# A tuned hybrid decoder layer: first-stage copies a tile ahead, a third buffer for sample states, gate weights split ahead, two FFN sums in other homes

## The chip, the cores and the metric

The kernel runs on one core of one Trainium2 chip. The metric is the device time of one execution in microseconds (us). The core has TensorE (PE: matmuls, and PEld: its weight loads), VectorE (DVE), ScalarE (ACT) and GpSimd (POOL), which compute, and SyncE (SP), which here only issues DMAs. POOL and ACT issue DMAs too. The instructions of one engine run in the order in which the program lists them; engines wait for each other through semaphores.

## What is computed

The reference is one inference step of one decoder layer, for a prompt of 512 new tokens and for 8 samples of one token each, with D = 2048, all in float32:

```
proj = rmsnorm(x, norm_mix_g) @ w_in      # columns: bg, cg, h (1024 each), q, k (512 each),
                                          # v, og (1024 each), glr (16)
ya = bg * causal_conv3(cg * h)            # 1024 channels
logf = log_sigmoid(glr @ gate_w2 + gate_b) / 16
S_t = diag(exp(logf_t)) S_{t-1} + k_t^T v_t ;  o_t = q_t S_t      # 4 heads, dk 128, dv 256
yb = rmsnorm(o, gla_norm_g) * silu(og)
x = x + concat(ya, yb) @ w_out
u, v = split(rmsnorm(x, norm_ffn_g) @ w_up)                       # 5632 channels each
x = x + (silu(causal_conv3(u) + b) * v) @ w_down
y = rmsnorm(x, final_norm_g)
```

The samples start from given states (two rows of each convolution, one S per sample and head), the prompt from zero states. The outputs are y and the new states.

## The kernel before, in words

**Layout.** Activations lie transposed, features on the 128 partitions, T = 520 tokens (512 of the prompt, 8 samples) along the row. A feature tile of x is a 128 x 520 block; there are 16 (KD). Every float32 operand of a matmul is split into two parts, hi = the value rounded to the reduced type fp32r (ACT) and lo = the rest (DVE), and a product is three matmuls: hi·hi, hi·lo, lo·hi. Weights come in pieces of 128 x 1024 floats (`load`, L98, on SP's queue; `parts`, L106, makes hi with ACT at L110 and lo with DVE at L111). The pools for raw, hi and lo pieces have three buffers each. `tmp()` (L91) gives one of eight temporaries. A `group` (L170) is one output tile of the projection: two pieces, 96 matmuls, and between quarters of it a `tick()` that emits one step of queued work.

**Order.** The instructions are placed on the engines by a scheduler. `InOrder` (L57) fixes their order in a region to the order of the program text: PE, DVE and ACT, and POOL or SP where they are named. In the first stage it holds PE, DVE, ACT and POOL; from L1575 on, POOL and SP as well. In between, the scheduler chooses.

**First stage (L276 to L491).** x arrives by rows and is transposed tile by tile. `x_tile(k)` (L367) transposes tile k on PE into one of two PSUM buffers, copies it to a temporary (ACT for k < 4, then DVE, L374 and L376), splits it with the norm's weight (L379 or L381, through `split`, L120, instructions at L125 and L126) and stores the copy to `xT_d` (L382, on SP). The loop at L434 runs over the 16 tiles: the matmuls of tile k for head 0's k and q columns, then `x_tile(k + 2)`. Beside it the squares of x are summed (tile column 0 on POOL and DVE, L448 and L449, the others on ACT, L451; the samples' in four pieces, L457), and the low-rank gate's weights, the states' rows and the parameters are loaded. Behind the loop stand the row norms (L467 to L470), `state_columns` (L417, eleven small transposes at L420 and four copies), the gate's matmuls over 12 tiles, the norms spread over partitions into R (L478 to L486), the gate over the other 4 tiles, and the masks for the heads (`make_masks`, L255, on POOL).

**Heads and convolution tiles (L740 to L1060).** For each of four heads: groups for k, q and v (two tiles), then a convolution tile of three groups (`conv_tile`, L755). The attention of a head (`gla_head`, L816) runs in steps at the ticks of later groups. Seven levels give the scores (L923 takes a level's product L, made by POOL, ACT and DVE). `sample_pair` (L884) loads two samples' states (`s0`, two buffers, L886) and their v rows, updates the states (L896) and stores them; `sample_out` (L905, matmul at L909) uses them two steps later. At the end of a head stands the norm of its output: a sum over partitions, a logarithm and an exponential on ACT, and a Newton step of four operations (`newton`, L237), on POOL for heads 0 to 2 and on DVE for head 3. In `conv_tile` the product z is made on POOL for tiles 0 to 2 (L765). After an odd tile, `mixed_done` (L745) forms sums of the tile and the even one before it, splits them and stores them.

**Gate (og), mix, output and FFN stages.** Two og groups follow (L1588 to L1619). Then all products use a scheme of seven products of half tiles (order 1, 5, 6, 2, 7, 3, 4) in place of eight; the sums of activations that it needs are `forms`, kept in 16 home slots, each a pair of hi and lo tiles (`form`, L648). 9 mix groups, 8 output groups ("wo"), 44 "up" and 20 "down" groups follow, each of seven products. `begin` (L1132) and `load_rest` load weights, `prepare` (L1143) splits a product's weights two products ahead (L1158 and L1162). During the last output group, earlier computed sums of the residual are loaded back (`load_sum`, L1534, on SP) and split in half steps set by `split_sums` (L1541); the loads are issued at the products listed at L1701. The first product of the up groups needs PSUM banks that the output groups' sums have just left (L1444 reads the last).

## Time and profile before

| | us |
|---|---|
| median of 3 runs | 2208.77 |
| the runs | 2207.36, 2208.77, 2214.17 |
| profiled execution | 2213.88 |
| its span on the core | 2212.1 |
| mean granted TensorE clock | 0.991 |

The profile is of one execution. A group row names line, engine, operation, what is written and read, count, then busy us and mean ns. A wait row says which line waited for which, with the total in us, the number of waits and the longest. A timeline row has the start in us, the duration, the engine, and in brackets the idle time ahead of it with what ended it; an engine with q is its queue of issued DMAs. A windows row has the length of the window, the busy us of PE, PEld, DVE, ACT and POOL with counts of instructions, the granted clock as a share of full speed, the share of time in which the 16 DMA engines moved data, and GB/s. A DMA row has its count, the size, and the median us from issue to landing. The clock of TensorE is granted by a throttle; 0.50 means half speed.

### The profile page before, as it was taken

How to read it: one execution, taken by the hardware profiler on the slowest of the kernel's cores; microseconds unless marked ns; L12 is line 12 of the kernel's file. 1: busy time of each engine (PE TensorE's matmuls, PEld its weight loads, DVE VectorE, ACT ScalarE, POOL GpSimd, SP SyncE). 2: the span in 40 equal slices, each digit the busy share in tenths (PEclk: the TensorE clock that was granted, in tenths of full speed). 3: DMA queues.
4: the chain of work that ended last, by engine and by line, in shares of the span. 5: the costliest groups of instructions: out<-in, count | busy, mean ns of one | idle time of the engine just before them, and what ended most of it. 6: DMA issues, size and time to landing. Idle time of an engine off the chain costs nothing.

```text
span 2212.1 us, 43799 instructions
## 1 busy us (share of the span) xinstructions
PE 2161.8 (98%) x17751; PEld 2136.8 (97%) x17751; DVE 1734.8 (78%) x2291; ACT 1112.8 (50%) x1629; POOL 444.6 (20%) x620
## 2 busy tenths in 40 slices
PE   7999999999999998999999999999999999999997
PEld 6999999989999998999999999999999999999997
DVE  5355463759887898989898899898988778888876
ACT  5345344335554476555555555555555553444444
POOL 3023241311223511112212121122121310010000
PEclk9999999999999999999999999999999999999999
DMA  8344454367788998666667667666677877894734
GB/s 244 108 132 127 134 176 137 110 204 185 198 215 281 297 247 240 159 174 181 183 163 193 175 168 188 175 181 182 163 193 194 287 189 205 243 273 131 218 110 150
DMA packets 468151, 415.51 MB, mean 188 GB/s; under 512 B 21593, under 2 KB 426357, under 8 KB 467805
## 3 DMA queue, kind: packets, MB, share of 16 engines
q1 hardware_dynamic: 425201, 291.84, 46.2%
q0 software_dynamic: 41424, 118.64, 20.5%
q8 instruction: 139, 2.28, 0.4%
q10 hardware_dynamic: 1324, 2.23, 0.3%
q14 instruction: 63, 0.52, 0.1%
HBM read 299.45 MB, written 80.31 MB: 172 GB/s over the span
## 4 chain that ended last, share of the span: by engine, by line
PE 74%; DVE 4%; DMA 3%; issue 1%; SPq 1%; ACT 1%; ACTq 0%; DVEq 0%
PE mm L1182 34%; PE ms L1182 13%; PE x L1425 7%; PE y L1425 7%; PE mm L139 5%; PE e L1425 3%; PE f L1425 3%; DVE lo L1162 1%; DMA raw<-in_w_out_dram 1%; DMA raw<-in_w_down_dram 1%; DVE acc L1444 1%; DVE yl L123 1%; DVE s L1103 0%; DMA yl<-mt_d 0%; DMA yl<-t_d 0%
## 5 line engine op out<-in xcount | busy, mean ns | idle before, releaser
L1182 PE MATMUL mm<-yh,hi 128*128 128x260 f32 x1696 | 479.9, 283 | 0.7 <-DVE t L597 0.7
L1182 PE MATMUL mm<-yl,hi 128*128 128x260 f32 x1696 | 478.5, 282 | 0.4 <-DVE yl L123 0.4
L1182 PE MATMUL mm<-yh,lo 128*128 128x260 f32 x1696 | 478.2, 282 | 0.3 <-DVE lo L1162 0.3
L1158 ACT ACTIVATE hi<-raw 128x1024 fp32r<-128x1024 f32 x324 | 342.6, 1057 | 231.9 <-PE mm L1182 67.2
L1162 DVE TENSOR_TENSOR lo<-raw,hi 128x1024 fp32r<-128x1024 f32 x324 | 396.0, 1222 | 40.7 <-ACT hi L1158 40.2
L1162 DVE TENSOR_TENSOR lo<-s,hi 128x1024 fp32r<-128x1024 f32 x243 | 298.5, 1228 | 127.6 <-ACT hi L1158 122.3
L1158 ACT ACTIVATE hi<-s 128x1024 fp32r<-128x1024 f32 x243 | 256.8, 1057 | 216.2 <-DVE s L1103 79.8
L1182 PEld LDWEIGHTS mm<-yl,hi 128*128 128x128 f32 x1696 | 319.1, 188 | 0.9 <-DVE yl L123 0.9
L1182 PEld LDWEIGHTS mm<-yh,lo 128*128 128x128 f32 x1696 | 319.3, 188 | 0.6 <-DVE lo L1162 0.6
L1182 PEld LDWEIGHTS mm<-yh,hi 128*128 128x128 f32 x1696 | 318.7, 188 | 1.0 <-issue 0.9
L1182 PE MATMUL ms<-b,hi 128*128 128x260 f32 x1408 | 255.8, 281 | 0.0
L1182 PEld LDWEIGHTS ms<-b,hi 128*128 128x128 f32 x1408 | 216.8, 188 | 0.0
L1425 PE MATMUL x<-form,hi 128*128 128x260 f32 x1120 | 204.6, 283 | 3.0 <-issue 1.7
L1425 PE MATMUL y<-form,hi 128*128 128x260 f32 x1120 | 204.4, 282 | 0.6 <-DVE acc L1444 0.6
L1103 DVE TENSOR_TENSOR s<-s,raw 128x1024 f32<-128x1024 f32 x162 | 198.1, 1223 | 2.8
L1182 PE MATMUL ms<-b,lo 128*128 128x260 f32 x704 | 198.7, 282 | 0.0
L1425 PEld LDWEIGHTS x<-form,hi 128*128 128x128 f32 x1120 | 172.5, 188 | 3.5 <-issue 2.9
L1425 PEld LDWEIGHTS y<-form,hi 128*128 128x128 f32 x1120 | 172.6, 188 | 0.8 <-issue 0.8
L111 DVE TENSOR_TENSOR lo<-raw,hi 128x1024 fp32r<-128x1024 f32 x76 | 95.3, 1258 | 82.2 <-ACT hi L110 75.5
L1425 PE MATMUL y<-form,lo 128*128 128x260 f32 x560 | 158.2, 283 | 0.0
L1425 PE MATMUL x<-form,lo 128*128 128x260 f32 x560 | 158.1, 282 | 0.0
L110 ACT ACTIVATE hi<-raw 128x1024 fp32r<-128x1024 f32 x76 | 79.5, 1051 | 109.2 <-PE mm L139 101.6
(367 smaller groups left out, 5161.9 us busy)
## 6 DMA issues: line engine op xcount, KB each, us to landing
raw<-in_w_up_dram SPq DMA_DIRECT2D x176, 512.0 KB, 4.0
raw<-in_w_down_dram SPq DMA_DIRECT2D x96, 512.0 KB, 6.7
raw<-in_w_in_dram SPq DMA_DIRECT2D x92, 512.0 KB, 4.9
form<-f_d SPq DMA_DIRECT2D x126, 260.0 KB, 6.5
raw<-raw POOLq DMA_DIRECT2D x56, 512.0 KB, 5.4
f_d<-t POOLq DMA_DIRECT2D x80, 260.0 KB, 5.5
raw<-in_w_out_dram SPq DMA_DIRECT2D x32, 512.0 KB, 12.6
form<-g_d POOLq DMA_DIRECT2D x42, 260.0 KB, 7.7
```

What stands on the lines that cost most here:

```text
L110: nc.scalar.activation(hi, raw, AF.Copy)
L111: nc.vector.tensor_tensor(lo, raw, hi.bitcast(F32), op=ALU.subtract)
L123: nc.vector.tensor_tensor(lo, src, hi.bitcast(F32), op=ALU.subtract)
L139: nc.tensor.matmul(o, w, xx, start=first and i == 0, stop=last and i == 2)
L1103: return lambda: nc.vector.tensor_tensor(out, x, y, op=ALU.add)
L1158: nc.scalar.activation(his[i], src, AF.Copy)
L1162: nc.vector.tensor_tensor(los[i], src, his[i].bitcast(F32), op=ALU.subtract)
L1182: nc.tensor.matmul(st["bank"][b], w[:, k, :], x, start=b not in st["used"] and k == 0 and j == 0, stop=k == 7 and j == 2, skip_group_check ...
L1425: nc.tensor.matmul(ps[:, m, :], w[:, k, m * P : (m + 1) * P], x, start=b not in st["used"] and k == 0 and j == 0, stop=k == 3 and j == 2, ...
L1444: nc.vector.tensor_tensor(a, a, inner(bk[b]), op=op)
```

## The change

- First stage: `x_tile` becomes `x_copy` (transposes and copy) and `x_split` (store to `xT_d`, now on POOL and ahead of the split, and the split). From k = 3 on the loop issues the copy of tile k + 3 ahead of the split of tile k + 2.
- The squares: the last tile column's four squares are issued in pairs at k = 14 and 15; the samples' become one instruction over all 2048 columns, in place, at k = 13.
- Head 0's first v weights are loaded at k = 8 and 9; their splits stand at k = 12 and behind the row norms.
- `state_columns` moves behind the gate's last matmuls. The gate runs over 8 tiles ahead of the norms' spreading and 8 behind it (12 and 4 before).
- Heads: the Newton step and the product z are on DVE for all heads. `sample_load` is apart from `sample_pair`; a pair is loaded at the end of the step before, and `s0` has three buffers. The even convolution tile's result stays in the z pad and not in a tile `ye` of the heads' pool.
- At the last convolution tile the order of the program text begins to hold for POOL and SP there and not at L1575, and the first og group's two pieces are loaded and split ahead of that tile's evacuation and sums; `load_og` gives the other two.
- FFN sums: forms (5, 0) and (5, 1) go to home slots 14 and 15 and (7, 2) and (7, 3) to 0 and 1 (they were the other way round); the loads of (5, 0) and (5, 1) are issued at product 0 of the last output group and not at product 1; the split of (4, 2) is half a step earlier. In `load_form`, homes 0 and 7 of the down forms are exchanged.

```diff
+    def group(w, c0, acts, ws=None):
-        ws = [piece(w, k0, 8, c0, P) for k0 in (0, 8)]
+        ws = ws or [piece(w, k0, 8, c0, P) for k0 in (0, 8)]
...
+        def x_copy(k):
             ps = tps()
...
+            st = copies[k] = tmp()[:, :T]
...
+        def x_split(k):
+            st = copies.pop(k)
+            nc.gpsimd.dma_start(xT_d[k], st)
             if k < KD // 2:
...
-            nc.sync.dma_start(xT_d[k], st)
...
+            while upto < min(k + (3 if k < 3 else 4), KD):
+                x_copy(upto)
+                upto += 1
             if k + 2 < KD:
-                x_tile(k + 2)
+                x_split(k + 2)
...
+            elif c < 3:
+                square(c, t)
+            if k in (8, 9):
+                v0.append(load(w_in, (k - 8) * 8, 8, 4096, P))
+            if k == 12:
+                v0[0] = parts(*v0[0])
+            if k == 13:
+                nc.scalar.activation(xs, xs, AF.Square, accum_out=var[:NS, 4:5])
+            if k >= 14:
+                square(3, 2 * k - 28)
+                square(3, 2 * k - 27)
...
-        state_columns()
+        v0[1] = parts(*v0[1])
...
-        low_rank_gate(glr_ps, 0, 12)
+        low_rank_gate(glr_ps, 0, 8)
...
-        low_rank_gate(glr_ps, 12, 4)
+        low_rank_gate(glr_ps, 8, 8)
...
+        state_columns()
         make_masks(sp)
...
-        newton(out, v, t, eng)
+        newton(out, v, t, nc.vector if out is not R else nc.gpsimd)
...
+        if kind == "down" and home in (0, 7):
+            home = 7 - home
...
+    FFN_HOMES = {(5, 0): 14, (5, 1): 15, (7, 2): 0, (7, 3): 1}
...
-            k = {5: 0, 4: 4, 6: 8, 7: 12}[f] + g
+            k = homes.get((f, g), {5: 0, 4: 4, 6: 8, 7: 12}[f] + g)
...
-            eng = nc.gpsimd if j < NH - 1 else nc.vector
-            eng.tensor_tensor(z[:, 2:], cgr[:, :T], hr[:, :T], op=ALU.mult)
+            nc.vector.tensor_tensor(z[:, 2:], cgr[:, :T], hr[:, :T], op=ALU.mult)
...
             ps = group(w_in, j * P, xa)
+            if j == NH - 1:
+
+                in_order = InOrder(nc.gpsimd.engine, nc.sync.engine)
+                ws_og.extend([piece(w_in, k0, 8, 5120, P) for k0 in (0, 8)])
...
-                even[j] = ya = evp[0].tile([P, T], F32, tag="ye", name="ye")
+                even[j] = ya = z[:, 2:]
...
-                def sample_pair(b0):
-                    s0 = gp.tile([P, 2, DV], F32, tag="s0", name="s0", bufs=2)
+                def sample_load(b0):
+                    s0 = gp.tile([P, 2, DV], F32, tag="s0", name="s0", bufs=3)
...
+                    if i < 4:
+                        s0.append(sample_pair(2 * i, *loaded))
                     if 2 <= i < 6:
                         sample_out(2 * i - 4, s0.popleft())
-                    if i < 4:
-                        s0.append(sample_pair(2 * i))
+                    if i < 3:
+                        loaded = sample_load(2 * i + 2)
...
-    raws = [load_og(n) for n in range(3)]
-    ws = [parts(*raws[0])]
-    raws.append(load_og(3))
+    raws = [load_og(2), load_og(3)]
...
-    ws.append(parts(*raws[1]))
-    ps = new_mm()
-    span(ps, ws[0], xa, 0, 0, 8, KD)
-    ws.append(parts(*raws[2]))
-    span(ps, ws[1], xa, 8, 8, 8, KD)
-    ws.append(parts(*raws[3]))
+    ps = new_mm()
+    span(ps, ws_og[0], xa, 0, 0, 8, KD)
+    ws = [parts(*raws[0])]
+    span(ps, ws_og[1], xa, 8, 8, 8, KD)
+    ws.append(parts(*raws[1]))
...
-        for n in (5, 5.5, 6.5, 7, 7.5, 8.5, 9, 9.5, 10):
+        for n in (5, 5.5, 6.5, 7, 7.5, 8, 9, 9.5, 10):
...
-                    1: ((5, 0), (5, 1)), 2: ((5, 2),), 3: ((4, 0), (4, 1)), 4: ((4, 2),),
+                    0: ((5, 0), (5, 1)), 2: ((5, 2),), 3: ((4, 0), (4, 1)), 4: ((4, 2),),
```

More of the change, by code (lines that the diff above doesn't have):

```diff
@@ L365, in trunk_kernel @@
         nc.vector.tensor_copy(gm, ps[:, :16])
-        def x_tile(k):
+        copies = {}
+        def x_copy(k):
             ps = tps()
@@ L427, in state_columns, with square @@
                 )
-        x_tile(0)
+        def square(c, t):
+            nc.scalar.activation(
+                tmp()[:, :512], xc[c][:, t, :], AF.Square,
+                accum_out=part[:, t, 3 + c : 4 + c],
+            )
+        x_copy(0)
+        x_split(0)
         warm(8)
         ws = [parts(raws[0], 8)]
-        x_tile(1)
+        x_copy(1)
+        x_split(1)
+        v0 = []
+        upto = 2
         in_order()
@@ L535, in rsqrt_sums, with rsqrt_rest @@
         return pss
[L537 removed]
+    def rsqrt_rest(pss, n, out):
         v, t = tmp()[:, :T], tmp()[:, :T]
@@ L742, in trunk_kernel @@
             slots[n] = yt1
-        even, evp = {}, [None]
+        even = {}
         def mixed_done(k, y):
@@ L936, in gla_head @@
                 Ls.append(level(LEVELS[1]))
+                loaded = sample_load(0)
                 yield
@@ L1012, in gla_head @@
                     yield
-                late = h == NH - 1
-                store = nc.gpsimd if late else nc.sync
+                store = nc.gpsimd if h == NH - 1 else nc.sync
                 store.dma_start(new_gla_p[0, 0, h], S)
@@ L1023, in gla_head @@
                 yield
-                rsqrt_wide(sq[:, :T], DV, ro[:, :T], nc.vector if late else nc.gpsimd)
+                rsqrt_wide(sq[:, :T], DV, ro[:, :T])
                 yield
@@ L1050, in trunk_kernel @@
                 for d in range(2):
-                    ps = group(w_in, 4096 + h * DV + d * P, xa)
+                    ps = group(w_in, 4096 + h * DV + d * P, xa, None if h + d else v0)
                     t = gp.tile([P, T], F32, tag="v", name="v", bufs=2)
@@ L1581, in trunk_kernel @@
     wxp = yctx.enter_context(tc.tile_pool(name="sums", bufs=2, side="right"))
-    og = [(5120 + j * P, k0) for j in range(2) for k0 in (0, 8)]
-    def load_og(n):
-        c0, k0 = og[n]
-        return load(w_in, k0, 8, c0, P)
-    raws = [load_og(n) for n in range(3)]
-    ws = [parts(*raws[0])]
-    raws.append(load_og(3))
+    raws = [load_og(2), load_og(3)]
     early = second_half(lambda m, k: mix_source(0, m, k))
@@ L1609, in trunk_kernel @@
     ps = new_mm()
-    span(ps, ws[2], xa, 0, 0, 8, KD)
+    span(ps, ws[0], xa, 0, 0, 8, KD)
     prepare(0)
@@ L1613, in trunk_kernel @@
         x()
-    span(ps, ws[3], xa, 8, 8, 8, KD)
+    span(ps, ws[1], xa, 8, 8, 8, KD)
     prepare(1)
@@ L1665, in trunk_kernel @@
             if kind == "wo" and at[0] == 1:
+                homes.update(FFN_HOMES)
                 if not ssq:
```

34 lines of the change are left out of this document (11 added, 23 removed).

## The prediction, made blind

> **What bounds the kernel now.** I read the page first, then the waits of the matmul engine, then the windows, and last the timeline around each long wait.
>
> ```profile
> span 2212.1 us, 43799 instructions
> PE 2161.8 (98%) x17751; PEld 2136.8 (97%) x17751; DVE 1734.8 (78%) x2291; ACT 1112.8 (50%) x1629; POOL 444.6 (20%) x620
> ```
>
> TensorE sets the time, and no matmul is removed here. Only its idle time, and time at a low clock, can be won. The waits (total, times, longest):
>
> ```profile
> PE mm L139 <- ACT hi L110: 7.9, 2, 5.4
> PE mm L1182 <- ACT hi L1158: 6.0, 1, 6.0
> PE mm L139 <- ACT xh L125: 3.8, 3, 2.4
> PE ms L909 <- DVE s L896: 3.4, 2, 2.2
> PE ms L923 <- DVE L L866: 2.7, 1, 2.7
> PE mm L139 <- ACT bh L125: 1.8, 1, 1.8
> ...
> PE mm L139 <- DVE xl L126: 1.4, 3, 0.8
> ```
>
> The windows give busy us of each engine, then the granted clock (PEclk):
>
> ```profile
> 11.00:59.60 48.60, 40.54 (x266) 35.26 (x266) 31.24 (x51) 29.12 (x64) 12.72 (x37) 0.93 0.77 240
> 50.77:54.18 3.41, 3.41 (x16) 3.06 (x16) 2.62 (x4) 2.13 (x6) 0.00 (x0) 0.50 0.99 262
> 204.37:207.78 3.41, 3.41 (x19) 3.41 (x18) 3.41 (x6) 1.43 (x4) 2.67 (x4) 0.50 0.09 31
> 224.84:228.25 3.41, 3.41 (x15) 2.96 (x14) 3.41 (x6) 0.63 (x1) 1.53 (x2) 0.50 0.26 81
> 310.18:313.59 3.41, 3.41 (x14) 2.51 (x13) 3.41 (x7) 0.54 (x2) 1.89 (x1) 0.50 0.28 86
> 463.78:470.60 6.82, 5.61 (x24) 5.31 (x25) 4.51 (x5) 3.03 (x4) 3.75 (x6) 0.50 0.81 220
> 491.00:511.50 20.50, 19.07 (x154) 18.37 (x153) 20.38 (x30) 12.48 (x21) 1.10 (x2) 1.00 0.66 172
> 850.00:2192.00 1342.00, 1338.45 (x11160) 1335.92 (x11158) 1153.50 (x1459) 696.49 (x975) 214.49 (x296) 1.00 0.69 188
> ```
>
> From 850 us on TensorE is busy 1338 of 1342 us at full clock: nothing is to be won there, and time won ahead of it passes through. One matmul takes 1342 / 11160 = 0.12 us there. Ahead of it stand a few waits, and short ones are followed by a stretch of 3.41 us in which the engine is busy at half clock. Each such stretch costs 3.41 x 0.5 = 1.7 us more; the one at 463.78 costs 5.61 x 0.5 = 2.8. A wait that goes takes its stretch with it: that is my reading, since the stretches stand where the waits stand.
>
> [...]
>
> **First stage.** The rows, in order of time:
>
> ```profile
> 47.20 1.06 ACT L110 ACTIVATE hi<-raw 128x1024 fp32r<-128x1024 f32 x1 [1.37 <-DMA raw<-in_w_in_dram]
> 48.93 0.51 PE L139 MATMUL mm<-xh,hi 128*128 128x260 f32 x2 [2.36 <-ACT xh L125]
> 58.65 0.62 ACT L451 ACTIVATE t<-xc 128x512 f32<-128x512 f32 x1
> 59.77 0.90 PE L420 MATMUL tp<-idn,frow 64*128 64x64 f32 x11
> 62.47 0.17 DVE L241 TENSOR_TENSOR rs<-rs,rs 128x5 f32<-128x5 f32 x1
> 66.42 1.05 PE L478 MATMUL tp<-idn,rs 128*128 128x128 f32 x8
> 71.07 0.39 PE L139 MATMUL mm<-bh,hi 128*128 128x260 f32 x1 [1.18 <-DVE k L500]
> ```
>
> Waits for xh, xl and bh are 3.8 + 1.4 + 1.8 = 7.0, and the stretch at 50.77 adds 1.7. The worst (2.36) is a v weight split that stands in ACT's queue ahead of tile 12's split and waits 1.37 for its load. In the change its place is fixed behind tile 14's split, its load is issued four tiles ahead of it, and SP no longer carries the 16 stores of x; this wait, its xl follower and the stretch should go. With the copy a tile ahead, the chain transpose, copy, split loses its first two links, and with them the other xh waits (3.8 - 2.4 = 1.4 in two) and xl waits should go. The bh wait is at tile 4, whose copy is not ahead yet (that starts at k = 3); I let 0.8 of 1.8 go, because the next tile's transposes now fill part of it. Sum 3.8 + 1.4 + 0.8 + 1.7 = 7.7.
>
> What is late next: the row norms. They were ready at 62.47 + 0.17 and wanted at 66.42, a slack of 3.8. The cover shrinks by four gate tiles (16 matmuls x 0.12 = 1.9) and the state transposes (0.9), leaving 1.0; two of the last four squares (0.62 each, row 58.65) run later, 1.2. So 0.2 is lost, at most 1.5. The four sample squares become one instruction on all 2048 columns, beside the matmuls: nothing. The moved transposes fall at the wait of 1.18 before the v group: they can cover it (gain 0.9), or their copies can stand ahead of DVE's evacuation (a loss of about the same, 2.6 with a stretch); I take zero. I take 7.5; bounds 4 and 9.5.
>
> The stores go through POOL instead of SP. Behind them on POOL stand the four products of tile column 0 and then the masks, in order; DVE's row sums wait for the products.
>
> ```profile
> f_d<-t POOLq DMA_DIRECT2D x80, 260.0 KB, 5.5
> 460.24 0.54 POOL L641 DMA_DIRECT2D g_d<-t  x1
> ```
>
> 16 issues x 0.54 = 8.6 us of POOL over some 45 us: covered. The masks (most of the 12.72 us of POOL in the window 11.00 to 59.60) start only behind the last store, so they end about when the gate sums end; zero taken, up to 2 us if the next stage's memory waits for them. A temporary stays taken until its store has landed, 5.5 us in the row.
>
> [...]
>
> **Samples and heads.**
>
> ```profile
> 185.25 1.05 POOL L238 TENSOR_TENSOR t<-t 128x520 f32<-128x520 f32 x1 [8.57 <-ACT t L543]
> ...
> 189.34 1.31 POOL L241 TENSOR_TENSOR t<-t 128x520 f32<-128x520 f32 x1
> 190.68 2.96 DVE L1028 SCALAR_TENSOR_TENSOR o<-o,par,t 128x520 f32<-128x520 f32 x2 [3.31 <-POOL t L241]
> 219.15 1.03 SPq L886 DMA_DIRECT2D s<-in_state_gla_dram  x2
> 223.61 0.88 DVE L896 SCALAR_TENSOR_TENSOR s<-s,asm,vb 128x256 f32<-128x256 f32 x2 [3.97 <-issue]
> 452.53 0.70 DVE L238 TENSOR_TENSOR t<-t 128x520 f32<-128x520 f32 x1 [9.91 <-ACT t L543]
> ```
>
> The Newton step of heads 0 to 2 takes POOL from 185.25 to 190.65, 5.4 us, and DVE stands still behind it. On DVE it is four operations of about 0.7, 2.8 us: 2.6 earlier, which is the wait of 2.7 at the next head's first level. It goes with its stretch: 4.4. The product for z (0.7) joins DVE and leaves POOL.
>
> The state pair at 223.61 was loaded at 219.15, because its buffer was the first pair's. With a third buffer and loads a step ahead both L909 waits go: 2.2 + 1.7 and 1.2 + 1.7 = 6.8. Together 11.2. The fourth pair still reuses a buffer and still queues behind weight loads on SP, so I hold back one wait of 0.5 and a stretch: 9.0, bounds 4.5 and 11.2. Keeping the even tile in the z pad frees the memory for the third buffer; the pad is next written two tiles later: nothing.
>
> **Gate weights.**
>
> ```profile
> 463.88 2.94 ACT L110 ACTIVATE hi<-raw 128x1024 fp32r<-128x1024 f32 x3
> 466.20 0.37 SPq L100 DMA_DIRECT2D raw<-in_w_in_dram  x1
> 479.92 0.38 SPq L1099 DMA_DIRECT2D raw<-in_w_in_dram  x1
> 486.52 1.06 ACT L1158 ACTIVATE hi<-raw 128x1024 fp32r<-128x1024 f32 x1 [5.67 <-DMA raw<-in_w_in_dram]
> ```
>
> TensorE waits 5.4 for splits that stand behind the last tile's sums on ACT and DVE. Split ahead, they are there in time: 5.4 + 2.8 = 8.2 at this place. Next late is the mix stage. It begins where the window 491.00 begins; its first weights landed at 486.5, at the end of a line of loads on SP that began at 466.20, when the late split freed a buffer; DVE was then full (20.38 of 20.50 us). TensorE would now come 8.2 earlier, but this line and DVE's work behind it only as much earlier as the loads start. They still need the memory of the heads, which is given back at about the time of the last tile's stores (460.24 above): 466.20 - 460.24 = 6.0 earlier, if nothing else holds them. I take 5.5; bounds 2 (only the one load is out of the line) and 9.6 (8.2 and the 20.50 - 19.07 = 1.4 that TensorE idles in the window behind it).
>
> **FFN sums.**
>
> ```profile
> 828.77 2.03 SPq L1538 DMA_DIRECT2D yl<-t_d  x2
> 836.92 0.64 ACT L122 ACTIVATE yh<-yl 128x520 fp32r<-128x520 f32 x1 [2.61 <-DMA yl<-t_d]
> 837.60 0.70 DVE L123 TENSOR_TENSOR yl<-yl,yh 128x520 fp32r<-128x520 f32 x1 [1.11 <-ACT yh L122]
> 844.96 0.69 DVE L1444 TENSOR_TENSOR acc<-acc,y 128x520 f32<-128x520 f32 x1
> ```
>
> The wait of 6.0 ends when DVE has read the last sums (844.96 + 0.69), which frees the banks. ACT stood 2.61 for the first loaded sum. In the other homes this load may go one product earlier, but on SP it passes only one store. And DVE is full from 837.60 on, idle only 1.11 before. So 1.0 goes, bounds 0 and 3 (1.1 and a stretch).
>
> **The sum.** 7.5 + 9.0 + 5.5 + 1.0 = 23.0. The profiled execution took 2213.9 (span 2212.1 and 1.8 around it), 5.1 above the median of 2208.8; it would come to 2190.9, and the median to 2186.
>
> **The rivals.**
>
> *The mix stage takes the gate's gain back.* For it: the 5.67 us that ACT waits at 486.52 for a load. Against: the line of loads lost its first member and the wait for it. Gain 23.0 - 5.5 = 17.5: 2191.
>
> *The copies are not ahead.* There are two PSUM buffers for the transposes, so the second of two copies may wait for DVE, and TensorE with it. Against: DVE is busy only 31 of 48.6 us there. The first stage gives nothing: 15.5, 2193.
>
> *The stretches are not the waits' doing.* If the clock falls for another reason than these short waits, the stretches at 50, 204, 224 and 310 us stay, 4 x 1.7 = 6.8. For it: they start up to 1.8 us behind a wait's end (48.93, 50.77). Against: no such stretch stands in the 1342 us without waits. Gain 16.2: 2193. [...]
>
> *DVE becomes the heads' bound.* Newton and z put 2.8 + 0.7 us more on DVE in each of four heads, beside its level products, which TensorE awaits (L923). Against: DVE is not full there. One wait of 2.7 with its stretch in each head returns 4 x 4.4 = 17.6: gain 5.4, 2203.
>
> *Slower: temporaries run out.* There are eight; a tile takes two, so one must be free after four tiles. A tile now takes 48.6 / 16 = 3.0 us. If stores through POOL held theirs for 19 us, a tile would take 4.8, 1.8 x 16 = 29 us more; with the other parts' 15.5 the time is 2222. Break-even is at about 16 us. Against: they land in 5.5.
>
> **How the numbers follow.** 0.3% is 6.6 us, about what a measurement of this kernel can tell. Chances: forecast 0.62 (its own range 2176 to 2198, from the bounds: gains of 33.3 and 10.5), mix 0.13, copies 0.08, stretches 0.04, DVE 0.08, slower 0.05. Faster by over 0.3%: 0.62 + 0.13 + 0.08 + 0.04 = 0.87; within: 0.08; slower: 0.05. The range goes to 2201, most of the way to the DVE case.
>
> **What would show it.** Right: no L125 or L126 wait above 1 us after tile 4, no half clock at about 42 to 46; no L909 wait and none at the second head's first L923; the og sums follow the last tile's without a gap; the first mix product waits 0 to 3 us; the wait at the first FFN product is still 4 to 6. Wrong: a wait on a POOL store or on DVE's row sums in the first stage, a wait over 2 us at the v group or in any head, or a first mix product that waits over 6 us.

## The result and the profile after

| | us | runs |
|---|---|---|
| before | 2211.24 | 4 (2207.36 to 2214.17) |
| changed | 2195.28 | 4 (2192.52 to 2195.78) |
| ratio | 0.9926, 95% interval 0.9906 to 0.9947 | |

The change is faster by 16.0 us; 23.0 were forecast. The profiled execution of the changed kernel took 2195.78. Its page, the span and the engines:

```profile
span 2194.0 us, 43790 instructions
PE 2155.7 (98%) x17751; PEld 2133.0 (97%) x17751; DVE 1738.9 (79%) x2305; ACT 1112.9 (51%) x1623; POOL 432.3 (20%) x621
```

The same matmuls run, TensorE's busy time is 6.1 us shorter, and the rest of the 18.1 us between the two spans are waits that are gone. Most of the 6.1 is time at half clock: up to the tail (the last 70 us of the span) TensorE was busy 26.34 us in such stretches and is now busy 16.49, half of the difference is 4.9. The waits of TensorE in the changed kernel follow (line waited for; total, times, longest); rows that are much as before are left out. L1217 is the old L1182, L1193 and L1197 the old L1158 and L1162, L956 the old L923, L517 the old L500, L1460 the old L1425:

```profile
PE mm L1217 <- ACT hi L1193: 7.1, 2, 5.0
PE mm L139 <- ACT hi L110: 2.9, 1, 2.9
PE mm L139 <- DVE bl L126: 2.1, 3, 0.9
PE mm L139 <- DVE k L517: 1.5, 1, 1.5
PE mm L1217 <- DVE lo L1197: 1.4, 3, 0.8
PE y L1460 <- DVE lo L1197: 1.1, 1, 1.1
PE ms L956 <- DVE L L896: 0.9, 2, 0.7
```

Gone are the waits for xh and bh, for L909's sums, and that of the og sums for `hi` at L110, 5.4 (the other of that row, at the start, is 2.9 now). Two things are new: waits for bl (2.1), and a second wait for `hi` at L1193 with one for `lo` at L1197 right behind it. The timeline of TensorE shows where it still waits: at the first v group, twice in the first product of the mix stage, at the first mix form, at the first up product, and at L139 behind the down groups.

```profile
64.95 0.39 PE L139 MATMUL mm<-bh,hi 128*128 128x260 f32 x1 [1.51 <-DVE k L517]
470.08 0.39 PE L1217 MATMUL mm<-bh,hi 128*128 128x260 f32 x1 [2.10 <-ACT hi L1193]
471.34 0.39 PE L1217 MATMUL mm<-bh,lo 128*128 128x260 f32 x1 [0.75 <-DVE lo L1197]
659.45 0.36 PE L1460 MATMUL x<-form,hi 128*128 128x260 f32 x1 [1.69 <-issue]
827.15 0.56 PE L1217 MATMUL mm<-bh,hi 128*128 128x260 f32 x1 [4.96 <-ACT hi L1193]
2125.39 0.36 PE L139 MATMUL mm<-bh,hi 128*128 128x264 f32 x1 [0.83 <-issue]
```

The same places in the kernel before (the v group, at 71.07, is shown in the prediction):

```profile
677.00 0.48 PE L1425 MATMUL x<-form,hi 128*128 128x260 f32 x2 [1.69 <-issue]
845.80 0.56 PE L1182 MATMUL mm<-bh,hi 128*128 128x260 f32 x1 [6.04 <-ACT hi L1158]
2142.04 0.36 PE L139 MATMUL mm<-bh,hi 128*128 128x264 f32 x1 [0.83 <-issue]
```

These places cut the span into pieces that can be compared, however far the whole has shifted. Each kernel was profiled a second time in the experiments (b_again, a_again); the second number in each cell is from there.

| from, to | before | changed | gain of the means | forecast |
|---|---|---|---|---|
| start, first v group | 71.07, 69.08 | 64.95, 63.54 | 5.8 | 7.5 |
| v group, first mix form (heads, og, mix start) | 605.93, 606.01 | 594.50, 592.70 | 12.4 | 14.5 |
| to the first up product | 168.80, 168.50 | 167.70, 167.46 | 1.1 | 1.0 |
| to L139 behind the down groups | 1296.24, 1296.00 | 1298.24, 1297.45 | -1.7 | 0 |
| to the end of the span | 70.10, 70.05 | 68.66, 68.65 | 1.4 | 0 |

Sum: 19.0 in the profiles, where the medians differ by 16.0. The profiled executions of before (2213.88 and 2211.35) lie 2.6 and 1.8 above the medians of their groups of runs (2211.24 and 2209.54); those of the changed kernel (2195.78 and 2191.51) lie 0.5 above and 1.3 below theirs (2195.28 and 2192.81). On average that is 2.2 + 0.4 = 2.6 of the 3.0.

Two rows scatter by themselves. At 11 us TensorE waits for its first weights (`hi` at L110), 2.5 and 0.4 us in the two profiles of before and 2.9 in both of the changed kernel; in its variants below it is 0.5 to 2.9. So the first row is good to about 2 us. The last piece takes 68.15 to 70.0 in these variants, so its 1.4 is not clear of the scatter.

Last, the slow clock. In the windows of the changed kernel around the v group (busy us of PE, PEld, DVE, ACT, POOL, then the granted clock) the second row has 3.41 - 1.90 = 1.5 us of idle TensorE, and the next 3.41 us are at half clock; the fourth row is the stretch behind the first mix product:

```profile
59.00:62.29 3.29, 3.29 (x30) 3.29 (x29) 1.93 (x3) 0.00 (x0) 3.03 (x7) 1.00 0.55 143
62.29:65.70 3.41, 1.90 (x20) 1.62 (x19) 2.98 (x10) 0.00 (x0) 2.34 (x9) 1.00 0.80 195
65.70:69.11 3.41, 3.41 (x18) 3.41 (x18) 0.37 (x2) 0.00 (x0) 0.00 (x0) 0.50 0.70 225
471.89:475.30 3.41, 3.41 (x18) 3.41 (x17) 3.38 (x5) 2.25 (x4) 0.00 (x0) 0.50 1.07 350
```

The stretches at 50.77, 204, 224, 310 and 463.78 are gone; these two, 1.7 us each, are new. Of the others, the one at the start lasts 6.83 us and not 3.41 (at 11.09, before at 13.22), and the one at the first up product 3.41 and not 6.83 (at 826.88, before at 842.66).

### The profile page after: what moved, and what is told of

Read it like the earlier page. It is cut to its first block, busy times and chain, and to the rows that moved or that the text cites. A ratio compares the mean times of both kernels' runs of the same rounds, so it can differ in the third digit from the quotient of the medians.

```text
span 2194.0 us, 43790 instructions
## 1 busy us (share of the span) xinstructions
PE 2155.7 (98%) x17751; PEld 2133.0 (97%) x17751; DVE 1738.9 (79%) x2305; ACT 1112.9 (51%) x1623; POOL 432.3 (20%) x621
## 3 DMA queue, kind: packets, MB, share of 16 engines
q8 instruction: 139, 2.28, 0.4%
## 4 chain that ended last, share of the span: by engine, by line
PE 59%; DMA 3%; DVE 1%; issue 1%; ACT 0%; ACTq 0%; SPq 0%; POOL 0%; DVEq 0%; POOLq 0%
PE mm L1217 28%; PE ms L1217 11%; PE x L1460 6%; PE y L1460 6%; PE f L1460 2%; PE e L1460 2%; PE mm L139 2%; DMA form<-f_d 1%; DMA ssq<-fh 1%; DMA x_d<-acc 1%; DMA raw<-in_w_down_dram 0%; PE ms L1789 0%; DVE lo L1197 0%; DMA yl<-t_d 0%; DVE yl L123 0%
## 5 line engine op out<-in xcount | busy, mean ns | idle before, releaser
L1217 PE MATMUL mm<-yh,hi 128*128 128x260 f32 x1696 | 479.5, 283 | 0.7 <-DVE t L614 0.7
L1217 PE MATMUL mm<-yl,hi 128*128 128x260 f32 x1696 | 478.7, 282 | 0.9 <-DVE yl L123 0.8
L1217 PE MATMUL mm<-yh,lo 128*128 128x260 f32 x1696 | 478.7, 282 | 0.6 <-DVE lo L1197 0.6
L1193 ACT ACTIVATE hi<-raw 128x1024 fp32r<-128x1024 f32 x324 | 342.5, 1057 | 238.0 <-PE mm L1217 69.0
L1197 DVE TENSOR_TENSOR lo<-raw,hi 128x1024 fp32r<-128x1024 f32 x324 | 395.2, 1220 | 47.0 <-ACT hi L1193 46.4
L1197 DVE TENSOR_TENSOR lo<-s,hi 128x1024 fp32r<-128x1024 f32 x243 | 298.3, 1228 | 127.9 <-ACT hi L1193 122.6
L1193 ACT ACTIVATE hi<-s 128x1024 fp32r<-128x1024 f32 x243 | 256.9, 1057 | 217.3 <-DVE s L1138 83.3
L1217 PEld LDWEIGHTS mm<-yl,hi 128*128 128x128 f32 x1696 | 319.1, 188 | 1.5 <-DVE yl L123 1.5
L1217 PEld LDWEIGHTS mm<-yh,lo 128*128 128x128 f32 x1696 | 319.4, 188 | 1.0 <-DVE lo L1197 1.0
L1217 PEld LDWEIGHTS mm<-yh,hi 128*128 128x128 f32 x1696 | 318.8, 188 | 1.1 <-issue 0.9
L1217 PE MATMUL ms<-b,hi 128*128 128x260 f32 x1408 | 255.9, 281 | 0.0
L1217 PEld LDWEIGHTS ms<-b,hi 128*128 128x128 f32 x1408 | 216.8, 188 | 0.0
L1460 PE MATMUL x<-form,hi 128*128 128x260 f32 x1120 | 204.8, 283 | 3.2 <-issue 1.9
L1460 PE MATMUL y<-form,hi 128*128 128x260 f32 x1120 | 204.4, 282 | 0.0
L1217 PE MATMUL ms<-b,lo 128*128 128x260 f32 x704 | 198.7, 282 | 0.0
L1460 PEld LDWEIGHTS x<-form,hi 128*128 128x128 f32 x1120 | 172.4, 188 | 4.1 <-issue 3.2
L1460 PEld LDWEIGHTS y<-form,hi 128*128 128x128 f32 x1120 | 172.5, 188 | 0.1
L1460 PE MATMUL y<-form,lo 128*128 128x260 f32 x560 | 158.3, 283 | 1.1 <-DVE lo L1197 1.1
L1460 PE MATMUL x<-form,lo 128*128 128x260 f32 x560 | 158.2, 282 | 0.0
L1217 PEld LDWEIGHTS ms<-b,lo 128*128 128x128 f32 x704 | 132.4, 188 | 0.0
```

Source lines behind the costliest of these rows:

```text
L1193: nc.scalar.activation(his[i], src, AF.Copy)
L1197: nc.vector.tensor_tensor(los[i], src, his[i].bitcast(F32), op=ALU.subtract)
L1217: nc.tensor.matmul(st["bank"][b], w[:, k, :], x, start=b not in st["used"] and k == 0 and j == 0, stop=k == 7 and j == 2, skip_group_check ...
L1460: nc.tensor.matmul(ps[:, m, :], w[:, k, m * P : (m + 1) * P], x, start=b not in st["used"] and k == 0 and j == 0, stop=k == 3 and j == 2, ...
```

## The experiments

Twelve runs were made in three groups, each group beside runs of the kernel before on its chip. Two theories stood at the start: each part's gain stands where its waits stood and passes through; or what the first stage, the heads or the og sums win is lost again behind them, above all at the mix stage. The first group undoes one part of the change at a time.

**u_first**: the first stage as before.

```diff
-        def x_copy(k):
-        def x_split(k):
+        def x_tile(k):
...
-        low_rank_gate(glr_ps, 8, 8)
+        low_rank_gate(glr_ps, 12, 4)
```

> The changed kernel with the first stage as it was before (one x_tile, stores of x on SP, the v pieces and the state columns in their old places); all else as changed. Theory (each part's gain stands where its waits stood, and passes through): the waits for xh, xl and bh come back, 5 to 7 us in all, and the first v group starts near 71.0 and not at 64.95, 6.1 us later; behind it nothing else changes, no L909 wait, no gap ahead of the og sums, and the first mix product still waits 2 to 3. Time 4.4 to 7.8 us above the changed kernel (the 6.1, less or more a stretch of half clock of 1.7): 2199.7 to 2203. Rival (the lead of this stage is lost again behind it, because the heads or the mix stage wait for loads whose start does not move with it): the v group starts 6 us later but the mix stage starts within 2 us of the changed kernel's 470, and the time is 2195 to 2197.

2197.78 (2195.81 to 2198.61, 5 runs), ratio 0.9946 (0.9933 to 0.9958). The v group starts at 68.81, 5.3 later than in the second profile of the changed kernel and 3.9 later than in the first; 6.1 were expected. From there to the first mix form it takes 593.19, between the changed kernel's 592.70 and 594.50: nothing of the lead is lost behind. The waits for xh, xl and bh are back with 2.1 + 2.0 + 1.4 = 5.5. By the ratio to before (0.9925 for the changed kernel, below) the part is worth 0.0021 x 2209 = 4.6 us, within the 4.4 to 7.8 expected; the time itself lies below the 2199.7 to 2203 named, as the changed kernel's does in its second group (2192.81). The rival falls.

**u_newton**: Newton step and z of heads 0 to 2 on POOL.

```diff
-                rsqrt_wide(sq[:, :T], DV, ro[:, :T])
+                rsqrt_wide(sq[:, :T], DV, ro[:, :T], nc.vector if late else nc.gpsimd)
...
-            nc.vector.tensor_tensor(z[:, 2:], cgr[:, :T], hr[:, :T], op=ALU.mult)
+            eng.tensor_tensor(z[:, 2:], cgr[:, :T], hr[:, :T], op=ALU.mult)
```

> The changed kernel with the Newton step and the product z of heads 0 to 2 back on POOL; third sample buffer and early sample loads stay. Theory: the wait at the second head's first level product comes back, 2.7 us, and with it a stretch at half clock of 1.7 if the wait fills more than about 1.2 us of one 3.41 us window: 2.7 to 4.4 us above the changed kernel, 2198 to 2199.7; no L909 wait. Rival 1 (the level wait came from the sample pair ahead of it on DVE, not from POOL): no wait over 1 us there, within 1 us of 2195. Rival 2 (DVE gets 3.5 us of room in each head and other waits go): 1 to 3 us faster than the changed kernel.

2199.77 (2196.11 to 2202.65, 5 runs), ratio 0.9957 (0.9944 to 0.9971). The level wait came back, and a second one behind it:

```profile
194.17 0.43 PE L957 MATMUL ms<-L 128*128 128x64 f32 x1 [2.67 <-DVE L L897]
206.44 0.32 PE L957 MATMUL ms<-L 128*128 128x64 f32 x1 [1.36 <-DVE L L897]
```

The stretch behind the first lasts two windows of the grid, and TensorE is busy in all of it:

```profile
194.25:201.07 6.82, 6.82 (x32) 6.82 (x33) 6.79 (x10) 3.73 (x7) 4.10 (x5) 0.50 0.37 120
207.91:211.32 3.41, 3.41 (x17) 3.22 (x16) 1.65 (x3) 2.50 (x4) 1.40 (x3) 0.50 0.17 59
```

From the v group to the first mix form it takes 600.81, 8.1 more than the changed kernel's 592.70 (both without a slow stretch behind the v group): 2.67 + 1.36 - 1.0 (what L956 waits there in the changed kernel) = 3.0 of waits, and (6.82 + 3.41) x 0.5 = 5.1 of slow clock. That these two make up the 8.1 is partly luck: the stretch at the mix stage is longer as well (6.83 us at 474.15, and 3.41 in a_again), which costs 1.4, and small terms take that back. By the ratios the part is worth 0.0032 x 2209 = 7.1. Forecast were 4.4. Against the rivals: the waits are POOL's doing, and nothing got faster for DVE's room. DVE waits 11.9 us for POOL in these heads, and its last step takes longer: the group row of that step, u_newton first, then the changed kernel (busy, mean ns, then idle before).

```profile
L1065 DVE SCALAR_TENSOR_TENSOR o<-o,par,t 128x520 f32<-128x520 f32 x8 | 7.3, 947 | 11.9 <-POOL t L241 11.9
```

```profile
L1063 DVE SCALAR_TENSOR_TENSOR o<-o,par,t 128x520 f32<-128x520 f32 x8 | 5.9, 753 | 0.0
```

The mean mixes two cases: seven of the eight operations take 0.75 us, and one takes 2.27, beside POOL's product for z. The kernel before has the same pair; the first of these rows is the second operation of the row at 190.68 in the prediction:

```profile
191.36 2.28 DVE L1028 SCALAR_TENSOR_TENSOR o<-o,par,t 128x520 f32<-128x520 f32 x1
191.75 1.32 POOL L765 TENSOR_TENSOR zpad<-t 128x520 f32<-128x520 f32 x1
```

So the Newton step and z both hold DVE up. They were put back together; what each brings alone was not tried.

**u_s0**: two sample buffers, loads in the pair's own step.

```diff
-                    s0 = gp.tile([P, 2, DV], F32, tag="s0", name="s0", bufs=3)
+                    s0 = gp.tile([P, 2, DV], F32, tag="s0", name="s0", bufs=2)
...
-                        s0.append(sample_pair(2 * i, *loaded))
+                        s0.append(sample_pair(2 * i))
```

> The changed kernel with two sample buffers and the loads inside the pair's own step, as before; the Newton step stays on DVE. Theory: two waits at L909's sums come back, about 2.2 and 1.2 us, each with a stretch at half clock of 1.7 only if it fills over about 1.2 us of one window of the 3.41 us grid: 3.4 to 6.8 us above the changed kernel, 2198.7 to 2202. Rival (the waits came from POOL's Newton step that delayed DVE, and the third buffer gives nothing): no wait at this line over 0.7 us, within 1 us of 2195.

2197.48 (2196.57 to 2202.0, 5 runs), ratio 0.995 (0.9937 to 0.9962). Only one of the two waits came back, and without a stretch; the windows row shows 3.41 - 1.93 = 1.5 us of idle ahead of a window at full clock:

```profile
213.10 0.40 PE L939 MATMUL ms<-s,qm 128*32 128x256 f32 x1 [1.56 <-DVE s L926]
```

```profile
209.61:213.02 3.41, 1.93 (x18) 1.80 (x16) 0.46 (x2) 1.58 (x2) 0.66 (x2) 1.00 0.92 290
213.02:216.43 3.41, 3.33 (x23) 2.66 (x24) 3.41 (x7) 0.00 (x0) 1.84 (x1) 1.00 0.24 77
```

From v group to mix form it takes 596.21: 3.5 more than the changed kernel, the lower end of what was expected (by the ratios it is 0.0025 x 2209 = 5.5). This wait is 1.56 of it, and the first mix product waits 2.68 where it waits 1.77 in a_again, 0.9 more; the remaining 1.0 is not placed. The other L909 wait stays away with two buffers, so it was not the buffer's; with POOL's Newton step and three buffers (u_newton) both stay away too. It seems to take both of the old parts.

**u_gate**: the og weights split behind the last tile.

```diff
-            if j == NH - 1:
-
-                in_order = InOrder(nc.gpsimd.engine, nc.sync.engine)
-                ws_og.extend([piece(w_in, k0, 8, 5120, P) for k0 in (0, 8)])
...
-    raws = [load_og(2), load_og(3)]
+    raws = [load_og(n) for n in range(3)]
```

> The changed kernel with the og weights loaded and split behind the last tile, as before. Theory (the mix stage's line of loads takes back what the og sums win): a wait of 5 to 5.5 us and a slow stretch (2.8) come back ahead of the og sums, and the waits of 2.1 and 0.8 and the slow stretch of 1.7 at the first mix product go; net 2.9 us above the changed kernel (bounds 2 and 4): 2198. Rival 1 (the wait at the first mix product has another cause and stays): 8.3 above, 2203.5. Rival 2 (all of the og gain is given back): within 1 us of 2195.

2196.39 (2193.93 to 2197.65, 5 runs), ratio 0.994 (0.9928 to 0.9953). The og wait is back:

```profile
448.80 0.59 PE L139 MATMUL mm<-bh,hi 128*128 128x260 f32 x1 [4.17 <-ACT hi L110]
```

A stretch of 6.83 us stands with it, and the first mix product waits for nothing. From v group to mix form it takes 597.39 against 594.50 in the first profile of the changed kernel (both with the slow stretch behind the v group): 2.9, as expected, and 0.0015 x 2209 = 3.3 by the ratios. So 2.9 of what the og sums won remains; the mix stage takes back the rest, as the theory had it.

The second group measures the changed kernel again and mends what its profile shows.

**a_again**: the changed kernel, unaltered.

> The changed kernel once more, unaltered: the base for the runs of this group, and a test of what brings the stretches at half clock. Theory (a fixed grid of 3.41 us per execution: a stretch follows a window of the grid in which TensorE was idle for about 1.3 us or more, and the grid lies elsewhere in each execution): the waits are the same (1.5 at the first v group, 2 to 2.7 and 0.7 at the first mix product, 4.9 at the first up product), but the starts of the slow stretches, divided by 3.4133, leave another remainder than in the first profile (0.85), and the stretch behind the v group's wait is there only if that wait lies in one window. Rival (a wait has its stretch or not, by its length): the same stretches at the same places as in the first profile, one at about 65.7 among them.

2192.81 (2191.51 to 2196.09, 5 runs), ratio 0.9925 (0.9912 to 0.9939). The wait at the v group is 1.51 us, as in the first profile, but without a stretch, because a border of the grid, at 62.66, lies within it:

```profile
59.25:62.66 3.41, 2.78 (x28) 2.51 (x26) 1.62 (x6) 0.00 (x0) 2.70 (x7) 1.00 0.91 255
62.66:66.08 3.42, 2.54 (x21) 2.54 (x22) 2.01 (x7) 0.00 (x0) 1.17 (x7) 1.00 0.73 220
66.08:69.49 3.41, 3.41 (x31) 3.41 (x30) 0.00 (x0) 0.11 (x1) 0.00 (x0) 1.00 0.20 68
```

Idle 0.6 in one window and 0.9 in the next: neither trips the clock. The three stretches ahead of the tail start at 11.46, 468.84 and 823.83; divided by 3.4133 each leaves 1.2, where the first profile has 0.85 and that of before 2.98. The grid reading holds, the rival falls. The first mix product waits 1.77 and 0.76, a little less than expected.

**p_mul**: POOL's four products ahead of the stores that they stood behind.

```diff
+        product(0)
+        product(1)
         x_copy(0)
         x_split(0)
...
         x_split(1)
+        product(2)
+        product(3)
```

> The changed kernel with POOL's four products of tile column 0 issued early: two ahead of the first store of a copy, two ahead of the loop. In the changed kernel each of them stands behind a store that waits for the copy, and so starts with VectorE's split of the same copy; that split takes 1.65 us there and not 0.49. Theory (VectorE and POOL hold each other up when both read two operands from memory): bl of tiles 2 to 5 takes about 0.5 again, the waits of 0.9, 0.9, 0.4 and 0.3 between 21 and 31 us go, the v group starts 2 to 2.5 earlier, time 2 to 2.5 us below the changed kernel of this group (up to 3.5 if a slow stretch goes as well). Rival (the split is slow for the descriptors of the store that POOL issues, not for the product): bl still takes about 1.6 at these tiles, and the time stays within 0.7.

The rows behind this experiment are of the changed kernel: VectorE's split of tile 4 beside POOL's product, and one split later without it.

```profile
24.91 0.57 POOL L381 DMA_DIRECT2D xT_d<-t  x1 [3.33 <-DVE t L377]
25.20 1.66 DVE L126 SCALAR_TENSOR_TENSOR bl<-t,gm,bh 128x260 fp32r<-128x260 f32 x1 [0.58 <-ACT bh L125]
25.50 1.05 POOL L465 TENSOR_TENSOR t<-x 128x512 f32<-128x512 f32 x1
26.91 0.39 PE L139 MATMUL mm<-bl,hi 128*128 128x260 f32 x1 [0.91 <-DVE bl L126]
32.21 0.47 DVE L126 SCALAR_TENSOR_TENSOR bl<-t,gm,bh 128x260 fp32r<-128x260 f32 x1
```

2189.34 (2187.42 to 2191.05, 5 runs), 3.5 below a_again in the same group, ratio 0.9906 (0.9893 to 0.9919). In p_mul the splits of tiles 2 to 5 take 0.49, and the hold-up has moved to tile 1, where nobody waits for it:

```profile
12.29 2.54 DVE L126 SCALAR_TENSOR_TENSOR bl<-t,gm,bh 128x260 fp32r<-128x260 f32 x1
12.50 2.04 POOL L443 TENSOR_TENSOR t<-x 128x512 f32<-128x512 f32 x2
23.55 0.49 DVE L126 SCALAR_TENSOR_TENSOR bl<-t,gm,bh 128x260 fp32r<-128x260 f32 x1 [0.58 <-ACT bh L125]
```

A split that takes 0.49 alone lasts 2.54, until both products are done. The v group starts at 60.94, 2.6 earlier (0.4 of it at the first wait for weights, 2.44 and not 2.86). The stores are still on POOL and the splits take 0.49, so it is not their descriptors: the rival falls. Whether it takes two operands on both sides, as the theory has it, was not tried by itself. One expected gain did not come: the wait of 0.4 at a transpose stays and is 0.59 here. It is for DVE's copy of an earlier tile (L377), not for the products.

**p_stf**: the states' copies on ACT.

```diff
-                nc.vector.tensor_copy(
+                nc.scalar.activation(
                     stf[:, g * 11 : (g + 1) * 11, :],
...
+                    AF.Copy,
```

> The changed kernel with the four copies of the states' columns on ACT and not on VectorE. Theory (the wait of 1.5 at the first v group is these copies, 1.08 in all, ahead of the evacuation of k on VectorE): the wait becomes about 0.5 (0.4 to 0.8), no stretch at half clock can follow it, time 1.0 us below the changed kernel where that had no stretch behind this wait, 2.7 where it had one. Rival (the wait is for R or the gate's last sums): the wait stays over 1.2 and the time the same.

2192.11 (2189.28 to 2193.59, 6 runs), 0.7 below a_again, ratio 0.9918 (0.9904 to 0.9931): within the noise, but the place shows it, 0.9 us of the wait are gone.

```profile
62.94 0.39 PE L139 MATMUL mm<-bh,hi 128*128 128x260 f32 x1 [0.58 <-DVE k L518]
```

**p_put**: the first mix product's weights ahead of six loads of sums on SP.

```diff
-    put = [load_sum(mt_d, f, g) for f in (5, 4) for g in range(1, 4)]
     ps = new_mm()
...
     load_rest(0)
+    put = [load_sum(mt_d, f, g) for f in (5, 4) for g in range(1, 4)]
```

> The changed kernel with the six loads of sums (yl from mt_d) issued behind the first mix product's weight loads on SP and not ahead of them. Theory (the first mix product waits because its weights, issued at 456, landed at 469, behind 1.6 MB of these loads and beside the stores of the last tile): its weights land before 466, the waits of 2.1 and 0.8 at the first mix product and the slow stretch behind them (1.7) go; the sums land later, and of the 4.5 some 1 to 2 come back as a wait for them at the second kind of products (y); net 2.5 to 4.5 us below the changed kernel. Rival (the line as a whole is short of DMA: whoever goes first, the last one comes as late): the waits move to the products on y, 2 to 3 us there, and the time stays within 1.

2190.28 (2189.72 to 2190.39, 4 runs), 2.5 below a_again, ratio 0.991 (0.9896 to 0.9924). In the changed kernel the load issued at 455.97 is split by ACT at 468.98, after a wait of 11.18:

```profile
455.97 0.38 SPq L1134 DMA_DIRECT2D raw<-in_w_in_dram  x1
468.98 1.06 ACT L1193 ACTIVATE hi<-raw 128x1024 fp32r<-128x1024 f32 x1 [11.18 <-DMA raw<-in_w_in_dram]
```

In p_put it is issued at 447.36 and there at 462.86; the loads of sums, now behind, cost a wait of 1.8 at the first product on y:

```profile
447.36 0.42 SPq L1134 DMA_DIRECT2D raw<-in_w_in_dram  x1
462.86 1.06 ACT L1193 ACTIVATE hi<-raw 128x1024 fp32r<-128x1024 f32 x1 [8.04 <-DMA raw<-in_w_in_dram]
474.14 0.39 PE L1217 MATMUL mm<-yh,hi 128*128 128x260 f32 x1 [1.81 <-ACT ms L1227]
```

The waits at the first mix product went, but the slow stretch did not: it now stands behind the wait on y, at 475.41. From the v group to the first mix form it takes 591.13, 1.6 less than in a_again; the rest of the 2.5 has no place in the profile. So the theory and the rival both hold in part. From issue to use the load still takes 462.86 - 447.36 = 15.5 us (13.0 in the changed kernel, and 6.6 in the kernel before, where it was issued at 479.92 and split at 486.52), so the loads in front were not all that slowed it. It runs beside the last tile's stores; whether these do it was not tried by itself.

**u_ffn**: the FFN part as before.

```diff
-    FFN_HOMES = {(5, 0): 14, (5, 1): 15, (7, 2): 0, (7, 3): 1}
...
-                    0: ((5, 0), (5, 1)), 2: ((5, 2),), 3: ((4, 0), (4, 1)), 4: ((4, 2),),
+                    1: ((5, 0), (5, 1)), 2: ((5, 2),), 3: ((4, 0), (4, 1)), 4: ((4, 2),),
```

> The changed kernel with the FFN part as before (homes of the sums, loads of two sums at product 1, split half a step later, homes 0 and 7 of the down forms not exchanged). Theory (the part moves about 1 us from the wait at the first up product and gives it back in the down groups, where the exchanged forms' loads come ahead of a weight load): the stretch from the first mix form's wait (659 in the changed kernel) to the first up product takes 168.3 to 169 and not 167.5, and the stretch from there to the wait at 2125 takes 1296.2 and not 1297.5 to 1298.2; net 0 to 0.5 slower than the changed kernel. Rival (the part is a gain of 1.0 and nothing is lost behind it): the second of these stays at 1297.5, 1 us slower.

2192.99 (2191.28 to 2194.01, 4 runs), ratio 0.9922 (0.9908 to 0.9935). From the first mix form to the first up product it takes 167.36, and from there to L139 behind the down groups 1298.25: as in the changed kernel in both. My theory and the rival fall. The part does nothing that can be seen. The other variants of the changed kernel take 166.2 to 168.8 for the first piece and 1297.0 to 1298.0 for the second, so the 1.1 won is within their scatter, and the 1.7 lost belongs to something that all of them share. Of the 1.7, 0.4 stands at a wait for yl (0.76 and 0.75 us in the changed kernel, 0.39 before) and 0.7 at the wait for `lo` at L1460, which before does not have (1.07 and 0.31); both are there in u_ffn too (0.67 and 0.74). Which edit it is stays open.

**b_again**: the kernel before, a second profile.

> The kernel before once more, unaltered, for a second profile. Theory (part of what its first profile showed was that one execution's: the late v weight load and where the grid of the clock lay): the waits that have their cause in the program return within 0.3 us (L923 2.7, L909 2.2 and 1.2, og sums 5.4, first up product 6.0, v group 1.2); the wait for the v weight split at 48.9 is 0.5 to 2.4, the stretches at half clock lie on another grid and one or two of the six are missing; the v group starts 67.5 to 70.5 and not at 71.07, time 2206 to 2211 and not 2213.9. Rival (the profile was as all executions are): v group 71.0, 2213.

2211.35, at the edge of the 2206 to 2211 that the theory named. The late v weight is no accident of one execution, as I had thought (47.08), one L909 wait is 3.35 and not 2.18, and the v group starts 2 us earlier:

```profile
47.08 0.39 PE L139 MATMUL mm<-xh,hi 128*128 128x260 f32 x1 [2.40 <-ACT xh L125]
69.08 0.39 PE L139 MATMUL mm<-bh,hi 128*128 128x260 f32 x1 [1.18 <-DVE k L500]
223.53 0.64 PE L909 MATMUL ms<-s,qm 128*32 128x256 f32 x1 [3.35 <-DVE s L896]
```

The stretches lie at 24.03, 47.92, 201.52, 222.0 (6.83 long), 460.93 and 839.81. The L909 wait at 309.81, 1.03 us, has none; in the first profile it was 1.18, in one window, and had one.

**u_store**: the stores of x's copies on SP again.

```diff
-            nc.gpsimd.dma_start(xT_d[k], st)
+            nc.sync.dma_start(xT_d[k], st)
```

> The changed kernel with the stores of x's copies on SP and not on POOL (still ahead of the split). Theory (POOL's products were late only because they stood behind these stores): the first products run at about 7.6 us again, VectorE's bl splits of tiles 2 to 5 take 0.5 and not 1.65, the waits of 0.9 and 0.9 go, v group 2 to 2.6 earlier than in the changed kernel with the same stretches, time 1.5 to 3.5 below it, ratio to before 0.9905 to 0.992. Rival (on SP the stores hold up the loads of weights and rows behind them): the splits are short again, but ACT waits 1 to 2 for the loads of w_in pieces and TensorE with it, and the time is the changed kernel's, ratio 0.992 to 0.9935.

2190.38 (2187.55 to 2192.39, 5 runs), ratio 0.9911 (0.9898 to 0.9925). The v group starts at 61.19. The group row of the splits, of the changed kernel and of u_store:

```profile
L126 DVE SCALAR_TENSOR_TENSOR bl<-t,gm,bh 128x260 fp32r<-128x260 f32 x8 | 8.5, 1064 | 9.8 <-ACT bh L125 9.8
```

```profile
L126 DVE SCALAR_TENSOR_TENSOR bl<-t,gm,bh 128x260 fp32r<-128x260 f32 x8 | 3.9, 488 | 9.8 <-ACT bh L125 9.8
```

A second way to take the products out of the splits' way has the same effect, so the cause is settled; and with the copies a tile ahead SP bears the stores without a new wait of TensorE for loads (its wait for `hi` at L110, the first weights, is 2.4 us, 2.9 in the changed kernel). The wait at a transpose is 0.58 here too.

**p_best**: p_mul, p_stf, and p_put with the second weight load left behind the six loads of sums.

```diff
     begin(0)
+    put = [load_sum(mt_d, f, g) for f in (5, 4) for g in range(1, 4)]
     load_rest(0)
```

> The changed kernel with three edits: POOL's products issued early, the states' copies on ACT, and the first mix product's weight load ahead of the six loads of sums (its second load, for a later product, stays behind them). Theory (the three gains stand at different places and add): 3.5 + 0.8 + 2.5 = 6.8 us below the changed kernel, ratio to before 0.9894 (0.988 to 0.991), v group at about 60.0 with a wait of 0.6, no wait over 0.7 at the first mix product, a wait of 1 to 1.8 at the first product on y. Rival (what the first two win is lost at the mix stage, where the line of loads ends at a fixed time): waits there grow by 2 to 3, ratio 0.991 to 0.992.

2185.27 (2184.59 to 2186.22, 4 runs) against 2209.54 for before in the same group, ratio 0.9888 (0.9874 to 0.9901): 24.3 us faster than before, and by the ratios 0.9925 - 0.9888 = 0.0037, 8 us, faster than the changed kernel, where 6.8 were expected: the gains add, and the rival falls. The v group starts at 60.12, the first mix product waits for nothing, and the wait on y is 1.4:

```profile
60.12 0.39 PE L139 MATMUL mm<-bh,hi 128*128 128x260 f32 x1 [0.58 <-DVE k L526]
469.46 0.39 PE L1226 MATMUL mm<-yh,hi 128*128 128x260 f32 x1 [1.42 <-ACT ms L1236]
```

## Why the prediction came out as it did

Direction and range held; the size was 23.0 and came out as 16.0. Of the 7 us, 4.0 are terms of the sum (19.0 in the profiles). The other 3 lie between the profiled executions and the medians, as worked out above: the sum was read off one profiled execution and carried over to the median in full. The time forecast, 2186, was missed by 9.3, because the kernel before, too, measured more in the end, 2211.24 and not 2208.8. By its number alone the result would fit two rivals better than the forecast, the stretches that stay (16.2) and the copies that are not ahead (15.5). That is chance: neither mechanism showed in that size, as told below.

- *First stage, 7.5; measured 5.8 in place, 3.9 and 5.3 by undoing it.* The waits for xh and the late v weight went, with the stretch at 50.77, as forecast. The step that failed is the stores' move: "16 issues x 0.54 = 8.6 us of POOL over some 45 us: covered". The issues were covered (16 of 0.54 to 0.70 us in the changed kernel, and nobody waits for one). But the four products behind them lost their early place and now start with the split of the same tile, which takes 1.65 in place of 0.49; the new waits for bl, 2.1, come from that. p_mul and u_store take it away and win 2.6 and 2.3 at the v group, 0.4 of each at the first wait for weights. The transposes moved to the v group were taken at zero; their copies made that wait 1.51 instead of 1.18, with a stretch in one profile of two.
- *The split beside a product.* The rows show what holds the splits up: one takes 1.66 us beside a product of 1.05 on POOL, 2.54 beside two of 2.04 and 0.47 alone. The prediction did not reckon with it, though its own row at 190.68 held a case: 2.96 us for two operations of 0.75 each, one of them beside POOL's product for z.
- *Heads, 9.0; measured 8.1 for the Newton step and z, 3.5 for the samples, 11.6 in all.* The waits went as forecast; the shares did not. The Newton step was sized at 4.4, and with z it brings 8.1 in one profile and 7.1 by the ratios, since with it goes a second level wait and more of the slow clock. The forecast gave the move of z no gain, but z on POOL held DVE up as well (2.28 us for an operation of 0.75). The sample loads were sized at 6.8, 4.6 with what was held back, and bring 3.5. Undone one at a time, these and the gate weights add to 14.5; in place, together, they bring 12.4. The parts overlap, and each ratio is known to about 0.0013, 2.9 us, so a share is good to 2 or 3 us.
- *Gate weights, 5.5; measured 2.9.* The og sums follow the last tile without a gap: the 5.4 and the slow stretch (2.8) went. The step that failed is that the mix stage's weights come as much earlier as their loads start. The load of the first mix product starts 479.92 - 455.97 = 24.0 earlier, more than TensorE needs: that product began at 490.86 without a wait and is now due at 470.08 - 2.10 = 467.98, 22.9 earlier. But from issue to use the load takes 13.0 us and not 6.6, so the weights come only 17.5 earlier; why it is slower stays open. The product waits 2.10 + 0.75, followed by a stretch, 1.7: 4.6 of the 8.2. That is the first rival (chance 0.13) in part; the 0 to 3 us named for this wait held.
- *FFN sums, 1.0; measured 0.* The wait did shrink from 6.0 to 4.4 to 5.0 in every variant, but it is 4.9 without this part as well.
- *The stretches.* The forecast read them as belonging to their waits. They do, but not one to one, as the next section but one tells. Half of TensorE's busy time in the stretches up to the tail is 13.2 and 11.1 us in the two profiles of before, 8.2 and 5.0 in those of the changed kernel: 5.5 gained, where the sum counted 1.7 + 1.7 + 3.4 - 1.7 = 5.1 ahead of the gate and 2.8 there. The rival in which they are not the waits' doing falls: the stretches at 204, 224 and 310 went with waits of 1.2 to 2.7 us.
- *The rival in which VectorE becomes the heads' bound* and the slow one of temporaries did not show: the longest level wait is 0.7, and there is no wait on a store. *The rival in which the copies are not ahead* shows in small, as the wait of 0.4 at a transpose for DVE's copy.

## What to carry to other kernels

Before an instruction or a DMA goes to another queue, look at what stands behind it there, and what that will now run beside: a covered issue can still push its followers onto a critical neighbour (here a split then took 1.65 us and not 0.49). A lead won ahead of a line of loads is only worth as much as the last of them arrives earlier, and a load that starts earlier may take longer (here one started 24.0 us earlier, took 13.0 us and not 6.6, and came 17.5 earlier). And before waits are taken off the median, ask how far the profiled execution lies above it; a second profile of the kernel before shows which waits and stretches return.

## What the hardware showed that was not expected

**The slow clock goes by a grid.** In the two profiles of each kernel and in u_newton the stretches start on one grid of 3.413 us, which lies elsewhere from execution to execution (the starts, divided by 3.4133, leave 2.98 before and 0.13 in b_again, 0.85 after and 1.2 in a_again, 3.1 in u_newton). Take the windows of that grid at full clock, up to the tail, in the first profile of each kernel: none with up to 1.11 us of idle TensorE was followed by a slow one; of the seven with 1.18 to 1.69 us two were, with 1.24 and 1.51; the nine with 1.91 us or more all were. A slow window was at times followed by a second one though TensorE hardly idled in it (u_newton at 194.25, busy all of the 6.82); when that happens stays open. So one wait of 1.51 us cost 1.7 more in two profiles (after, u_gate) and nothing more in others (a_again, u_newton). Also open: the wait of 1.69 for "issue" at the first mix form, with 1.60 us of idle TensorE in one window before and 1.69 after, had no stretch in either profile of either kernel.

**VectorE stands still beside POOL.** In the rows shown, a VectorE operation on two inputs in memory that meets a product on POOL ends 0.3 to 0.6 us behind that product: 0.49 becomes 1.65 or 2.54 us, and 0.75 becomes 2.28. By its recorded start it is the operation that began first, by 0.2 to 0.4 us, and it is held all the same; the rows do not show why. In a page this looks like a slow VectorE: its busy time grows, and only the mean of the group (1064 ns against 488) tells.
